# Row sums of squares by ScalarE's accumulating square on token-major loads, in a one-core decoder block

## The chip, the cores and the metric

The kernel runs on one core of a Trainium2 chip. The metric is the device time of one execution in microseconds (us). A core has five engines with queues of their own: PE (TensorE, matrix products), DVE (VectorE, elementwise), ACT (ScalarE, activations), POOL (GpSimd) and SP (which here only issues transfers). Transfers (DMA) are issued from SP, ACT or POOL and all run on the same 16 DMA engines. Each engine runs its instructions strictly in the order in which they stand in its queue.

## What is computed

One layer of a hybrid decoder block on 2048 tokens of 1024 channels: an RMS norm, one projection to 3080 columns, a pooling branch and a gated DeltaNet branch, an output projection with the residual, and a last RMS norm. The part that the change touches is the first norm:

```python
def rms_norm(x, w):
    xf = x.astype(jnp.float32)
    y = xf * lax.rsqrt(jnp.mean(xf * xf, axis=-1, keepdims=True) + NORM_EPS)
    return (y * w.astype(jnp.float32)).astype(x.dtype)

def reference(x, norm_w, w_in, ...):
    n = rms_norm(h, norm_w[layer])
    proj = jnp.einsum('bsd,de->bse', n, w_in[layer])
```

The scale of a token, one over the root of its mean square, is a factor of every projected column. So the kernel projects the unscaled x (times the norm's weight) and multiplies the scale into the results.

## The kernel before

**Tiling.** The tokens go in two blocks of 1024 (`b` = 0, 1), each in two halves of 512 (`hf` = 0, 1). x is loaded channel-major (`xT`: 128 channels on the partitions, 512 tokens along the row), as eight slices of a half in four transfers of 512 KB (`load_x`). Each slice, times the norm's weight, is split into a high part `nh` (rounded to the fast matmul type, on ACT) and a remainder `nl` (on DVE) by `split_x`. A projection (`project`) is eight steps `k`, each a triple of 512-column matmuls: `nh` and `nl` with the weight's high part `wh`, and `nh` with its low part `wl`. A projection of one weight tile over one half is 24 matmuls, a unit.

**Weights.** The first two weight tiles come with the first loads and are split on the engines. For each later tile POOL issues a transfer into `wh`, ACT makes a negated rounded copy in `wl` (L716), and POOL issues a second transfer that adds the weight to it (L717).

**The row scale.** `square_x` squares each slice on ACT; the squares are summed over the eight slices into `sacc`, the odd ones by DVE, the even ones by POOL (L533). `row_scale` then sums over the partitions: for each 128 tokens a matmul with one column of ones (`pss`, L538) puts the sum for each token on a partition. DVE adds the epsilon (`ms`, L542), POOL takes the power of -1/2 (`rstd`, L500), and DVE multiplies the 128x128 identity, which is loaded in `cst`, with each of the four scales (L549). `broadcast` multiplies these four diagonals by a matrix of ones (`psr`, L553): the scale of every token now stands on every partition, and ACT copies it to `rb` (L555). Every result of a projection is multiplied by `rb` when it leaves PSUM. A result that has no `rb` yet keeps its PSUM bank: three banks of pool `pp` and two of `pc` take the first five units.

**Gates.** Two more columns groups of the projection (`gate_rows`, `psba`) are scaled by `rb` on DVE (`ba`, L566) and transposed by PE (`tp`, L573), once for each half.

**What sets the order.** The program is traced in the order of slots that are written by hand (`at(slot, fn)`); the constants `L_...` are the offsets. A planner then lists all instructions again for each engine, with costs of its own for each operation and transfer (`costs`), and binds each engine to that order. Loads that are traced before `load_constants` are the opening: the planner sends them first, and reckons their landings one behind the other. SP keeps at most eight transfers under way: an issue waits until the eighth before it has landed.

The opening's loads on SP are the first half's `xT`, the weights, the second half's `xT`, and then the constants: `cst`, `wba` (the gate weights, from which `whl` is made), `pw`, and others.

Of the kernel before, what the change touches and what calls it, by code (L numbers as in the profile page):

```python
# [7 lines left out]
F32 = mybir.dt.float32  # L8
# [3 lines left out]
ALU = mybir.AluOpType  # L12
# [23 lines left out]
L_SPREAD, L_KK0 = 1.0, 4.5  # L36
L_CONV, L_SCAT, L_GAT, L_INV, L_FIN, L_POOL, L_GATE = 9, 8.4, 8.4, 28, 15.0, 12, 15
L_RB = (5.5, 4.25, 5.25, 4.25)
L_MIX, WARM = 90, 11
L_ROW, L_GROW, L_SUMS, L_DEC = 3.0, 2.5, 2, 4.0  # L40
L_KK, L_Q, L_QK, L_SPLIT, L_W = 1.5, 6.5, 1.5, 20, 30
L_ROW0, L_SQ1, L_SQB, L_X, L_GR0, L_GR, L_GCOL = (16.0, 18.0), 13.5, -40, 44, 21.5, 5.5, 2.75
# [44 lines left out]
class Planner:  # L87
# [34 lines left out]
    def costs(self, i, outs, ins):  # L122

        op, eng = i.opcode, i.engine.name
        n = 1
        for _, c in outs[0].bass_ap.ap[1:]:
            n *= c
        psum = any(a.bass_ap.tensor.name in self.psum for a in (*outs, *ins))
        if op == "DMACopy":
            kb = n * outs[0].bass_ap.ap[0][1] / 256  # L130
            if eng == "Pool":
                return 600, (2900 + 5.3 * kb if self.adds(i) else 2300 + 3.1 * kb)
            if type(outs[0].bass_ap.tensor).__name__ != "Tile" or outs[0].bass_ap.tensor.name.startswith(DRAM_TILES):
# [12 lines left out]
        if eng == "Activation":
            scaled = len(outs) > 1 or len(ins) > 1
            t = 170 + 0.6 * n if psum else 93 + 0.85 * n + 95 * scaled
            return t, t + 108
        if eng == "Pool":  # L150
            t = 600 if op == "TensorTensor" and n <= NC else {"TensorScalarAffineSelect": 620}.get(op, 0.95 * n if op == "Memset" else 2.5 * n + 20)
            return t, t + 30
        if op == "StreamTranspose":
            return 464, 450
        if op in ("TensorTensor", "TensorCopy"):
            t = 70 + 1.04 * n
        else:
            t = 125 + 1.05 * n if n >= P else 78 + n
        return t, t + 98
# [237 lines left out]
def hymba_kernel(  # L397
# [31 lines left out]
    def st(shape, dt, tag, bufs=1):  # L429
        return plan.tile(sp, shape, dt, tag, tag, bufs)  # L430
# [89 lines left out]
            out=nl[:, k], in0=xk, scalar=nw[:, k : k + 1], in1=nh[:, k], op0=ALU.mult, op1=ALU.subtract  # L520
        )

    def square_x(k, env):
        xk = env["x"][k // 2][:, k % 2]
        if k == 0:
            env["ss"] = ss = st([P, HALF], F32, "sacc", 2)
            nc.scalar.activation(ss, xk, AF.Square)
        else:
            ss = env["ss"]
            sq = st([P, HALF], F32, "acc", 3)  # L530
            nc.scalar.activation(sq, xk, AF.Square)
            eng = nc.vector if k % 2 else nc.gpsimd
            eng.tensor_tensor(out=ss, in0=ss, in1=sq, op=ALU.add)  # L533

    def row_scale(env):
        ps = plan.tile(pd, [P, HALF], F32, "pd", "pss", 2, True)
        for j in range(NCH):
            nc.tensor.matmul(  # L538
                ps[:, j : j + 1], env["ss"][:, j * P : (j + 1) * P], ones[:, 0:1], start=True, stop=True
            )  # L540
        v = st([P, NCH], F32, "ms", 2)
        nc.vector.tensor_scalar(  # L542
            out=v, in0=ps[:, 0:NCH], scalar1=1.0 / D, scalar2=EPS, op0=ALU.mult, op1=ALU.add
        )
        r = st([P, NCH], F32, "rstd", 2)
        rsqrt(r, v)
        env["dg"] = dg = st([P, NCH, P], F32, "sacc", 2)
        for j in range(NCH):
            nc.vector.tensor_scalar(out=dg[:, j], in0=ident, scalar1=r[:, j : j + 1], scalar2=None, op0=ALU.mult)  # L549
# [550 lines left out]
    for b in range(NB):  # L1100
# [21 lines left out]
        for hf in range(NHALF):  # L1122
            n[hf] = env = {}
            base = slot - (1 - hf) * 8 * PAIRED + 0.5
            for i in range(KT // 2):
                at(base - L_X if b else -79 + 8 * hf + i, load_x, b, hf, i, env)
            for k in range(KT):
                at(base + 0.1 + k * (8 * PAIRED - 2) / KT, split_x, k, env)
                at(base + (L_SQB if b else 4 + L_SQ1 * hf) + k * (8 * PAIRED - 2) / KT, square_x, k, env)
            base += 8 * PAIRED - 2  # L1130
            base += L_ROW if b else L_ROW0[hf]
            at(base, row_scale, env)
            at(base + L_RB[b * NHALF + hf], broadcast, env)
            env["slot"] = base + L_RB[b * NHALF + hf] + 0.1
        for hf in range(NHALF):
# [401 lines left out]
```

## Time and profile before

| | us |
|---|---|
| three timed runs | 944.51, 944.46, 942.41 (median 944.46) |
| the profiled execution | 943.07 |
| its span, first to last instruction | 941.4 |
| mean granted clock of PE | 0.996 |

Some of the costliest groups of instructions (line, engine, operation, out<-in, shapes, count, then busy us and mean ns):

```profile
L725 PE MATMUL ps<-nh,wh 128*128 128x512 f32 x768 | 325.8, 424 | 2.0 <-DVE sz L750 1.5
L716 ACT ACTIVATE wl<-wh 128x1024 fp32r<-128x1024 f32 x40 | 42.4, 1060 | 43.7 <-DMA wh<-in_w_in_dram 34.0
```

A group's last part is the idle time of the engine just before its instructions and what ended it. A wait's row names the instruction that waited, the one it waited for, and the microseconds in total, the number of times and the longest.

### The profile page before, as it was taken

The numbers are of one execution on the slowest core, as the hardware profiler recorded it, in microseconds if no ns is written. First come the engines' busy times: TensorE is split into PE (matmuls) and PEld (weight loads), VectorE is DVE, ScalarE is ACT, GpSimd is POOL, SyncE is SP. The second block draws the span as 40 slices with busy tenths as digits, with TensorE's granted clock in tenths as the row PEclk, the third lists the DMA queues.
The fourth block names the chain that finished last, engine by engine and source line by source line (L and its number), as shares of the span: only waits on it lengthen the run. The fifth ranks groups of instructions, "written<-read, shape, count | busy, mean of one in ns | idle before, by whom it ended". The sixth has DMA issues, their size and how long they took to land.

```text
span 941.4 us, 14710 instructions
## 1 busy us (share of the span) xinstructions
PE 916.7 (97%) x5226; PEld 739.4 (79%) x5226; DVE 618.2 (66%) x1637; ACT 467.0 (50%) x1209; POOL 187.5 (20%) x224
## 2 busy tenths in 40 slices
PE   8999999999999999999999999999999999999995
PEld 6678888878888877768877787888887788788884
DVE  7476867667758445855775775865844487976553
ACT  8348654464454245624944545545523435444442
POOL 3417210110111113312710121021011101012221
PEclk9999999999999999999999999999999999999998
DMA  8425574343433455434445344343248487376544
GB/s 291 103 60 108 135 170 109 63 99 87 96 100 75 134 168 151 95 74 90 95 96 123 63 91 95 73 101 98 63 110 255 127 229 227 127 187 163 152 111 123
DMA packets 82265, 115.81 MB, mean 123 GB/s; under 512 B 31888, under 2 KB 49552, under 8 KB 82192
## 3 DMA queue, kind: packets, MB, share of 16 engines
q0 software_dynamic: 17280, 56.89, 28.3%
q1 hardware_dynamic: 64480, 57.46, 19.9%
q8 instruction: 41, 0.67, 0.3%
q10 hardware_dynamic: 432, 0.53, 0.2%
q14 instruction: 32, 0.26, 0.1%
HBM read 92.83 MB, written 22.02 MB: 122 GB/s over the span
## 4 chain that ended last, share of the span: by engine, by line
PE 73%; issue 8%; DMA 6%; DVE 6%; POOL 2%; ACT 2%; SPq 1%; DVEq 0%; POOLq 0%; ACTq 0%
PE ps L725 14%; PE ps L727 14%; PE ps L726 14%; DMA wh<-in_w_in_dram 2%; PE psA L1391 2%; PE psA L1392 2%; PE psA L1390 2%; PE tp L817 2%; PE ch L1003 2%; PE ch L981 1%; PE ch L997 1%; PE ob L991 1%; PE ob L1007 1%; DMA dec<-in_xT_dram 1%; PE psC L1392 1%
## 5 line engine op out<-in xcount | busy, mean ns | idle before, releaser
L725 PE MATMUL ps<-nh,wh 128*128 128x512 f32 x768 | 325.8, 424 | 2.0 <-DVE sz L750 1.5
L726 PE MATMUL ps<-nl,wh 128*128 128x512 f32 x768 | 300.9, 392 | 2.2 <-DVE nl L519 2.2
L727 PE MATMUL ps<-nh,wl 128*128 128x512 f32 x768 | 301.5, 393 | 1.5 <-DMA wl<-in_w_in_dram 1.5
L727 PEld LDWEIGHTS ps<-nh,wl 128*128 128x128 f32 x768 | 144.2, 188 | 34.8 <-DMA wl<-in_w_in_dram 3.0
L725 PEld LDWEIGHTS ps<-nh,wh 128*128 128x128 f32 x768 | 145.0, 189 | 27.6 <-DVE sz L750 1.9
L726 PEld LDWEIGHTS ps<-nl,wh 128*128 128x128 f32 x768 | 145.2, 189 | 27.2 <-DVE nl L519 5.0
L739 DVE SCALAR_TENSOR_TENSOR acc<-u,cw,acc 128x512 f32<-128x512 f32 x144 | 109.7, 762 | 20.4 <-ACT acc L737 18.4
L708 POOL DMA_DIRECT2D wh<-in_w_in_dram x40 | 23.1, 578 | 295.2 <-PE ps L727 283.0
L734 DVE TENSOR_TENSOR u<-ps,rb 128x512 f32<-128x512 f32 x48 | 33.1, 689 | 56.5 <-PE ps L727 56.4
L717 POOL DMA_DIRECT2D wl<-in_w_in_dram x40 | 35.2, 880 | 163.8 <-ACT wl L716 116.6
L716 ACT ACTIVATE wl<-wh 128x1024 fp32r<-128x1024 f32 x40 | 42.4, 1060 | 43.7 <-DMA wh<-in_w_in_dram 34.0
L896 DVE TENSOR_TENSOR tmp<-Ai,X 128x60 f32<-128x60 f32 (+24 forms) x248 | 53.5, 216 | 9.4 <-DMA Ai<-blocks 3.1
L902 DVE TENSOR_TENSOR X<-X,tmp 128x60 f32<-128x60 f32 (+24 forms) x248 | 53.7, 216 | 6.6
L737 ACT ACTIVATE acc<-u,cw 128x512 f32<-128x512 f32 x48 | 34.9, 727 | 44.9 <-DVE u L734 43.9
L1010 ACT ACTIVATE sqj<-v 128x128 f32<-128x128 f32 x64 | 19.7, 308 | 62.2 <-DVE v L1008 61.0
L999 ACT ACTIVATE nv<-ch,sm 128x128 f32<-128x128 f32 x64 | 23.5, 368 | 33.9 <-PE ch L997 33.8
L1398 POOL DMA_DIRECT2D dec<-in_x_dram x23 | 20.2, 880 | 100.6 <-ACT dec L1397 58.9
L1004 DVE SCALAR_TENSOR_TENSOR state<-state,ex,ch 128x128 f32<-128x128 f32 x64 | 22.0, 344 | 22.1 <-PE ch L1003 21.2
L824 ACT ACTIVATE sqj<-tp 128x128 f32<-128x128 f32 x128 | 33.6, 278 | 4.4 <-PE tp L817 4.2
L993 ACT ACTIVATE o<-ob,ex 128x128 f32<-128x128 f32 x64 | 23.6, 369 | 20.4 <-PE ob L991 19.6
L1003 PEld LDWEIGHTS ch<-nv,kdec 128*128 128x128 f32 x128 | 19.6, 188 | 13.2 <-ACT nv L999 12.6
L750 DVE TENSOR_TENSOR szp<-ps,rb 128x512 f32<-128x512 f32 x16 | 11.0, 689 | 27.8 <-PE ps L727 27.8
(286 smaller groups left out, 1761.7 us busy)
## 6 DMA issues: line engine op xcount, KB each, us to landing
wh<-in_w_in_dram POOLq DMA_DIRECT2D x40, 512.0 KB, 4.0
wl<-in_w_in_dram POOLq DMA_DIRECT2D x40, 512.0 KB, 5.5
y_dram<-yt SPq DMA_DIRECT2D x32, 256.0 KB, 2.9
out_dram<-dec SPq DMA_DIRECT2D x14, 512.0 KB, 4.5
dec<-in_x_dram POOLq DMA_DIRECT2D x23, 256.0 KB, 4.1
Ai<-blocks SPq DMA_DIRECT2D x32, 128.0 KB, 2.7
yr<-y_dram SPq DMA_DIRECT2D x8, 512.0 KB, 4.4
dec<-in_xT_dram SPq DMA_DIRECT2D x7, 512.0 KB, 6.6
```

The source lines that it names most:

```text
L716: nc.scalar.activation(w["lo"], w["hi"].bitcast(F32), AF.Copy, scale=-1.0)
L717: nc.gpsimd.dma_start(w["lo"], w_in[et], accum_op=ALU.add)
L725: nc.tensor.matmul(ps, w["hi"][:, k], nh[:, k], start=(k == 0), stop=False)
L726: nc.tensor.matmul(ps, w["hi"][:, k], nl[:, k], start=False, stop=False)
L727: nc.tensor.matmul(ps, w["lo"][:, k], nh[:, k], start=False, stop=(k == KT - 1))
L734: nc.vector.tensor_tensor(out=ub[:, HALO:], in0=ps, in1=rb, op=ALU.mult)
L737: nc.scalar.activation(acc, ub[:, HALO:], AF.Copy, scale=cw[:, ci, CONV - 1 : CONV])
L739: nc.vector.scalar_tensor_tensor(out=acc, in0=ub[:, h0 + j : h0 + j + HALF], scalar=cw[:, ci, j : j + 1], in1=acc, op0=ALU.mult, op1=ALU.add,)
L824: nc.scalar.activation(junk, tp[:, j], AF.Square, accum_out=dst[:, c : c + 1])
L896: nc.vector.tensor_tensor(out=tmp[:, 0:n, 0:w], in0=Ai[:, j, j + 1 : BS].unsqueeze(1).to_broadcast([P, n, w]), in1=X[:, 0:n, j : j + 1].to ...
L902: nc.vector.tensor_tensor(out=X[:, 0:n, j + 1 : BS], in0=X[:, 0:n, j + 1 : BS], in1=tmp[:, 0:n, 0:w], op=ALU.subtract)
L1003: nc.tensor.matmul(ch[:, 2], e["kdec"][:, c], nv, start=True, stop=True)
```

## The change

The sums of squares are no longer made from the channel-major slices. x is loaded a second time, token-major: 128 tokens on the partitions and their 1024 channels along the row, 512 KB each (`load_rows`), four such loads for a half. ACT squares each in place and sums along the row in the same instruction (`square_rows`, `accum_out`), which leaves a token's sum on its partition, where the one-column matmul had put it. `square_x`, its additions and the matmuls `pss` are gone. `row_scale` keeps the epsilon and the power; the diagonals are a step of their own (`row_diagonal`).

In block 0 the row loads belong to the opening and use buffers that are free then (`ROW_TAGS`); one of them, `Ai`, is used by the first load of the first half and by the last of the second. In block 1 all eight go through one buffer (`yr1`), so each waits for the square of the one before. The slots are new too, and the planner's cost of a small power on POOL.

```diff
+ROW_TAGS = (
+    (("Ai",), ("At",), ("v0",), ("vT",)),
+    (("Tt", 2), ("Tt", 2), ("yr1",), ("Ai",)),
+)
...
-            t = 600 if op == "TensorTensor" and n <= NC else ...
+            t = 430 + 160 * n if op == "TensorTensor" and n <= NC else ...
...
-    def square_x(k, env):
-        xk = env["x"][k // 2][:, k % 2]
-        if k == 0:
-            env["ss"] = ss = st([P, HALF], F32, "sacc", 2)
-            nc.scalar.activation(ss, xk, AF.Square)
-        else:
-            ss = env["ss"]
-            sq = st([P, HALF], F32, "acc", 3)
-            nc.scalar.activation(sq, xk, AF.Square)
-            eng = nc.vector if k % 2 else nc.gpsimd
-            eng.tensor_tensor(out=ss, in0=ss, in1=sq, op=ALU.add)
+    def load_rows(b, hf, j, env):
+        env["xt", j] = xt = st([P, D], F32, *(ROW_TAGS[hf][j] if b == 0 else ("yr1",)))
+        t0 = b * TB + hf * HALF + j * P
+        nc.sync.dma_start(xt, x[t0 : t0 + P, :])
+
+    def square_rows(j, env):
+        if j == 0:
+            env["ms"] = st([P, NCH], F32, "ms", 2)
+        xt = env["xt", j]
+        nc.scalar.activation(xt, xt, AF.Square, accum_out=env["ms"][:, j : j + 1])
 
     def row_scale(env):
-        ps = plan.tile(pd, [P, HALF], F32, "pd", "pss", 2, True)
-        for j in range(NCH):
-            nc.tensor.matmul(
-                ps[:, j : j + 1], env["ss"][:, j * P : (j + 1) * P], ones[:, 0:1], start=True, stop=True
-            )
-        v = st([P, NCH], F32, "ms", 2)
...
+        v = env["ms"]
+        nc.vector.tensor_scalar(out=v, in0=v, scalar1=1.0 / D, scalar2=EPS, op0=ALU.mult, op1=ALU.add)
+        env["r"] = r = st([P, NCH], F32, "rstd", 2)
         rsqrt(r, v)
+
+    def row_diagonal(env):
         env["dg"] = dg = st([P, NCH, P], F32, "sacc", 2)
...
-                at(base + (L_SQB if b else 4 + L_SQ1 * hf) + k * (8 * PAIRED - 2) / KT, square_x, k, env)
...
-            at(base, row_scale, env)
+            for j in range(NCH):
+                at(base - L_XT + 4 * j if b else -70.5 + 8 * hf + 0.1 * j, load_rows, b, hf, j, env)
+                at(base - L_XT + 8 + 4 * j if b else 4 + 8 * hf + j, square_rows, j, env)
+            at(base - L_XT + 24 if b else base, row_scale, env)
+            at(base, row_diagonal, env)
             at(base + L_RB[b * NHALF + hf], broadcast, env)
```

What the planner makes of it shows in three places. First SP at the start of the program. Before (the names are those of the sections above; `dec`, `kdec`, `kT` are buffers that hold `xT` here, `qT` a weight):

```order
L703 DMA qT<-in_w_in_dram 128x512 x2
L513 DMA dec<-in_xT_dram 128x2x512
L513 DMA kdec<-in_xT_dram 128x2x512
L513 DMA kT<-in_xT_dram 128x2x512 x2
L481 DMA cst<-in_consts_dram 128x192
L481 DMA wba<-in_w_ba_dram 128x64
L481 DMA pw<-in_pool_w_dram 128x512
```

And with the change (its line numbers are those of the changed file; `in_x_dram` is x token-major):

```order
L703 DMA qT<-in_w_in_dram 128x512 x2
L517 DMA dec<-in_xT_dram 128x2x512
L530 DMA Ai<-in_x_dram 128x1024
L530 DMA At<-in_x_dram 128x1024
L530 DMA v_139<-in_x_dram 128x1024
L530 DMA vT<-in_x_dram 128x1024
L517 DMA kdec<-in_xT_dram 128x2x512
L517 DMA kT<-in_xT_dram 128x2x512 x2
L530 DMA Tt<-in_x_dram 128x1024 x2
L530 DMA yr_153<-in_x_dram 128x1024
L530 DMA Ai<-in_x_dram 128x1024
L485 DMA cst<-in_consts_dram 128x192
```

Four row loads stand between the first and the second load of the second half's `xT`, and four more between the last of these and `cst`.

Second, DVE in the opening. Before, from the first split of the second half on:

```order
L519 SCALAR_TENSOR_TENSOR nl<-dec,nw,nh 128x512 x2
L533 TENSOR_TENSOR sacc<-sacc,acc 128x512
L519 SCALAR_TENSOR_TENSOR nl<-kdec,nw,nh 128x512 x2
L519 SCALAR_TENSOR_TENSOR nl<-kT,nw,nh 128x512 x2
L542 TENSOR_SCALAR ms<-pss 128x4
L489 TENSOR_TENSOR whl<-wba,whl 128x8x8
L519 SCALAR_TENSOR_TENSOR nl<-kT,nw,nh 128x512 x2
L549 TENSOR_SCALAR sacc<-cst,rstd 128x128 x4
```

With the change:

```order
L523 SCALAR_TENSOR_TENSOR nl<-dec,nw,nh 128x512 x2
L540 TENSOR_SCALAR ms<-ms 128x4
L523 SCALAR_TENSOR_TENSOR nl<-kdec,nw,nh 128x512 x2
L523 SCALAR_TENSOR_TENSOR nl<-kT,nw,nh 128x512
L547 TENSOR_SCALAR sacc<-cst,rstd 128x128 x4
L523 SCALAR_TENSOR_TENSOR nl<-kT,nw,nh 128x512
L493 TENSOR_TENSOR whl<-wba,whl 128x8x8
L523 SCALAR_TENSOR_TENSOR nl<-kT,nw,nh 128x512
L763 TENSOR_TENSOR u<-ps,rb 128x512
```

The scale and the diagonals (`sacc<-cst,rstd`) have moved ahead of the last three splits. PE has 22 triples ahead of the first `psr` now, and had 21 and one group of `pss`. On POOL the first `wh` and `wl` transfers follow the first memsets now; before, an addition stood ahead of `wh`, and `wl` came behind three additions and the first power.

Third, DVE in block 1, up to the first `ba`. Before:

```order
L542 TENSOR_SCALAR ms<-pss 128x4
L770 TENSOR_TENSOR ps_s<-ps_s 128x513
L782 SCALAR_TENSOR_TENSOR acc<-ps_s,u 128x512
L549 TENSOR_SCALAR sacc<-cst,rstd 128x128 x4
L750 TENSOR_TENSOR szp<-ps,rb 128x512
L519 SCALAR_TENSOR_TENSOR nl<-dec,nw,nh 128x512 x2
L519 SCALAR_TENSOR_TENSOR nl<-kdec,nw,nh 128x512 x2
L519 SCALAR_TENSOR_TENSOR nl<-kT,nw,nh 128x512
L792 SCALAR_TENSOR_TENSOR yt<-acc,psc,szp 128x512
L519 SCALAR_TENSOR_TENSOR nl<-kT,nw,nh 128x512 x3
L566 TENSOR_TENSOR ba<-psba,rb 16x512
```

With the change:

```order
L770 TENSOR_TENSOR ps_s<-ps_s 128x513
L782 SCALAR_TENSOR_TENSOR acc<-ps_s,u 128x512
L750 TENSOR_TENSOR szp<-ps,rb 128x512
L523 SCALAR_TENSOR_TENSOR nl<-dec,nw,nh 128x512 x2
L523 SCALAR_TENSOR_TENSOR nl<-kdec,nw,nh 128x512 x2
L523 SCALAR_TENSOR_TENSOR nl<-kT,nw,nh 128x512
L792 SCALAR_TENSOR_TENSOR yt<-acc,psc,szp 128x512
L523 SCALAR_TENSOR_TENSOR nl<-kT,nw,nh 128x512 x3
L566 TENSOR_TENSOR ba<-psba,rb 16x512
```

The scale and the diagonals of this half are gone from this place; they stand some 60 rows earlier.

More of the change, by code (lines that the diff above doesn't have):

```diff
@@ L38 @@
 L_RB = (5.5, 4.25, 5.25, 4.25)
-L_MIX, WARM = 90, 11
+L_MIX, L_XT, WARM = 90, 60, 11
 L_ROW, L_GROW, L_SUMS, L_DEC = 3.0, 2.5, 2, 4.0
@@ L150, in costs @@
         if eng == "Pool":
-            t = 600 if op == "TensorTensor" and n <= NC else {"TensorScalarAffineSelect": 620}.get(op, 0.95 * n if op == "Memset" else 2.5 * n + 20)
+            t = 430 + 160 * n if op == "TensorTensor" and n <= NC else {"TensorScalarAffineSelect": 620}.get(op, 0.95 * n if op == "Memset" else 2.5 * n + 20)
             return t, t + 30
@@ L521, in split_x @@
         )
-    def square_x(k, env):
-        xk = env["x"][k // 2][:, k % 2]
-        if k == 0:
-            env["ss"] = ss = st([P, HALF], F32, "sacc", 2)
-            nc.scalar.activation(ss, xk, AF.Square)
-        else:
-            ss = env["ss"]
-            sq = st([P, HALF], F32, "acc", 3)
-            nc.scalar.activation(sq, xk, AF.Square)
-            eng = nc.vector if k % 2 else nc.gpsimd
-            eng.tensor_tensor(out=ss, in0=ss, in1=sq, op=ALU.add)
-    def row_scale(env):
-        ps = plan.tile(pd, [P, HALF], F32, "pd", "pss", 2, True)
-        for j in range(NCH):
-            nc.tensor.matmul(
-                ps[:, j : j + 1], env["ss"][:, j * P : (j + 1) * P], ones[:, 0:1], start=True, stop=True
-            )
-        v = st([P, NCH], F32, "ms", 2)
[L542 to L545, printed above, removed]
+    def load_rows(b, hf, j, env):
[7 more added lines that the diff above has]
+        nc.scalar.activation(xt, xt, AF.Square, accum_out=env["ms"][:, j : j + 1])
+    def row_scale(env):
+        v = env["ms"]
+        nc.vector.tensor_scalar(out=v, in0=v, scalar1=1.0 / D, scalar2=EPS, op0=ALU.mult, op1=ALU.add)
+        env["r"] = r = st([P, NCH], F32, "rstd", 2)
         rsqrt(r, v)
+    def row_diagonal(env):
         env["dg"] = dg = st([P, NCH, P], F32, "sacc", 2)
         for j in range(NCH):
-            nc.vector.tensor_scalar(out=dg[:, j], in0=ident, scalar1=r[:, j : j + 1], scalar2=None, op0=ALU.mult)
+            nc.vector.tensor_scalar(
+                out=dg[:, j], in0=ident, scalar1=env["r"][:, j : j + 1], scalar2=None, op0=ALU.mult
+            )
     def broadcast(env):
```

## The prediction

> **What bounds the kernel now.** The page comes first: busy times, then the chain that ended last.
>
> ```profile
> span 941.4 us, 14710 instructions
> PE 916.7 (97%) x5226; PEld 739.4 (79%) x5226; DVE 618.2 (66%) x1637; ACT 467.0 (50%) x1209; POOL 187.5 (20%) x224
> ...
> PE 73%; issue 8%; DMA 6%; DVE 6%; POOL 2%; ACT 2%; SPq 1%; DVEq 0%; POOLq 0%; ACTq 0%
> ```
>
> TensorE is busy for 97% of the span. Its instruction order is fixed, so work taken from it shortens the kernel, and work taken from the others does so only where TensorE waits. The list of TensorE's waits over the whole run says where:
>
> ```profile
> PE ps L726 <- DVE nl L519: 2.2, 5, 0.7
> PE tp L573 <- DVE ba L566: 1.9, 1, 1.9
> ```
>
> The first is the opening, where data arrives just in time. The second is the start of block 1. The change touches both places. So I read two stretches closely: 0 to 55 us and 389 to 410 us.
>
> **What leaves TensorE.** The one-column matmuls stand in the timeline as four groups. Two of them, one in each block, with the instruction that follows (start, duration):
>
> ```profile
> 22.16 0.94 PE L538 MATMUL pss<-ones,sacc 128*128 128x1 f32 x8
> 22.97 0.49 PE L725 MATMUL ps<-nh,wh 128*128 128x512 f32 x1
> ...
> 408.87 1.05 PE L538 MATMUL pss<-ones,sacc 128*128 128x1 f32 x8
> 409.78 0.48 PE L725 MATMUL ps<-nh,wh 128*128 128x512 f32 x1
> ```
>
> A group holds TensorE for 0.81 us (22.97 less 22.16) to 0.91 us; I take 0.81 for three and 0.91 for the last. All four would be 3.3 us if nothing else moved.
>
> **What the added loads do in the opening.** The queue of SP is the place to look. Windows of 4 to 16 us (columns: length, busy of PE, PEld, DVE, ACT, POOL, clock, DMA share, GB/s), and the issue and time to landing of the constants `cst`:
>
> ```profile
> 4.00:16.00 12.00, 9.92 (x38) 6.43 (x37) 9.61 (x14) 10.36 (x18) 2.30 (x2) 1.00 1.05 389
> ...
> 8.79 0.34 SPq L481 DMA_DIRECT2D cst<-in_consts_dram  x1
> cst<-in_consts_dram SPq DMA_DIRECT2D x1, 96.0 KB, 8.4
> ```
>
> The DMA engines are full (share 1.05) at 389 GB/s. The 96 KB of `cst` take 8.4 us because they land behind everything issued earlier: 8.79 + 8.4 = 17.2 us. In the changed order eight loads of 512 KB rows stand ahead of `cst`. They move 8 x 0.524 MB = 4.19 MB, and 4.19 / 0.389 = 10.8 us. Two transfers of POOL's queue also come before it now. Their rows:
>
> ```profile
> 14.20 0.75 POOL L708 DMA_DIRECT2D wh<-in_w_in_dram  x1
> ...
> 25.84 0.91 POOL L717 DMA_DIRECT2D wl<-in_w_in_dram  x1
> ...
> 27.00:32.00 5.00, 5.00 (x20) 2.81 (x21) 3.32 (x10) 3.90 (x7) 0.39 (x1) 1.00 0.75 133
> ```
>
> `wh` was issued at 14.20, behind an addition on POOL; with the additions gone it follows the memsets. Its 0.52 MB cost the others at most 0.52 / 0.389 = 1.3 us, and part of it overlapped `cst` already: +1.0. `wl` was issued at 25.84, after `cst`; it now follows ACT's first row square and so comes before it. At the full rate it costs 1.3 us. The window 27 to 32, which holds it and little else, shows 0.75 x 5 = 3.75 us of all engines for 0.67 MB, so up to 3.0 us for 0.52 MB. I take 1.9, nearer to the full-rate row because that one is from a full queue.
>
> `cst` lands at 17.2 + 10.8 + 1.0 + 1.9 = **30.9 us**, between 29.5 (both at 1.3 or less, rows a little faster) and 32.3 (1.3 and 3.0).
>
> The Trainium skill, "DMA: Bandwidth & Descriptors", section Specifications, gives about 358 GB/s as the limit of HBM for one core. At that figure the rows would take 11.7 us (an estimate from that page), 0.9 more. The 389 GB/s measured here is above it, so the measurement decides.
>
> **Who waits for `cst`.** The identity in `cst` is multiplied by the row scale into four diagonals, and these feed `psr`, the broadcast matmul:
>
> ```profile
> 25.90 0.89 DVE L549 TENSOR_SCALAR sacc<-cst,rstd 128x128 f32<-128x128 f32 x4 [0.27 <-POOL rstd L500]
> 26.94 1.10 PE L553 MATMUL psr<-sacc,ones 128*128 128x512 f32 x2 [0.26 <-DVE sacc L549]
> ...
> 53.31 0.39 PE L725 MATMUL ps<-nh,wh 128*128 128x512 f32 x1
> 53.54 0.39 PE L726 MATMUL ps<-nl,wh 128*128 128x512 f32 x1
> 53.76 0.39 PE L727 MATMUL ps<-nh,wl 128*128 128x512 f32 x1
> 54.08 0.42 PE L573 MATMUL tp<-cst,ba 16*128 16x16 f32 x4
> ```
>
> Before, the diagonals waited 0.27 us for `rstd` from POOL, with `cst` long there. Now the row scale is early and `cst` is late. `psr` follows the first diagonal by 26.94 - 25.90 = 1.04 us, so it starts at 30.9 + 1.04 = 31.9. Behind the diagonals on DVE stand three of the `nl` splits, `whl` and the first product with `rb`. On ACT, `whl<-wba` waits for the next constant, with a split, a square and the `rb` copy behind it. TensorE waits for all of these, but after `psr`, and they are 0.2 to 0.8 us each while `psr` and the three triples behind it run.
>
> TensorE has 22 triples (three matmuls of 512 columns) ahead of `psr` now, and had 21 and a `pss` group. Its matmuls start 0.23 us apart (53.31, 53.54, 53.76), so a triple takes 0.68 us. I compare at `tp`, the second transpose of gate rows, which has 43 triples ahead of it in both kernels. Before: 54.08 - 26.94 = 27.14 us from `psr` to it. Now one triple and one `pss` group fewer: 27.14 - 0.68 - 0.81 = 25.65, so 31.9 + 25.65 = 57.6. **Term 1: +3.5 us** (+2.1 to +4.9 by the bounds). The squares on ACT do not add to it: the four rows of the first half land ahead of the second half's `xT`.
>
> **The clock.** TensorE runs out of work at 21 to 26 us (22 triples from 6.06 on are 15 us, and its waits for `nl` add some), so it stands idle for 6 to 11 us. Rows of the end and of the start show what that does:
>
> ```profile
> 930.87 0.40 PE L1392 MATMUL psA<-Ai,wl 128*128 128x512 f32 x1
> 932.00:934.00 2.00, 0.00 (x0) 0.00 (x0) 0.90 (x3) 1.85 (x5) 0.00 (x0) 0.96 0.00 0
> 934.00:936.00 2.00, 0.00 (x0) 0.00 (x0) 1.61 (x4) 0.41 (x3) 1.60 (x2) 0.50 0.00 0
> ...
> 1.13 4.75 PE L465 MATMUL warm<-ones 128*128 128x128 f32 x22 [1.13 <-DVE mhalf L460]
> ...
> 6.39 0.40 PE L726 MATMUL ps<-nl,wh 128*128 128x512 f32 x1
> 6.79 0.50 PE L727 MATMUL ps<-nh,wl 128*128 128x512 f32 x1
> 7.21 0.50 PE L725 MATMUL ps<-nh,wh 128*128 128x512 f32 x1
> ...
> 10.25 0.39 PE L727 MATMUL ps<-nh,wl 128*128 128x512 f32 x1
> 10.48 0.40 PE L725 MATMUL ps<-nh,wh 128*128 128x512 f32 x1
> ```
>
> After the last matmul the granted clock falls to 0.50 within 3 us. At the start the matmuls follow each other in 0.40 and 0.42 us until 7.21, and in 0.23 by 10.48. The clock column reads 1.00 there all the same, so I go by the steps: TensorE was slow for 6.1 to 9.3 us from its first matmul at 1.13, and slow steps take twice the time: 3.0 to 4.6 us lost. After a gap in mid-run the price lies between 0 (the gate stays open) and 4.6; the nearest row says 3.0, the middle is 2.3. **Term 2: +2.7 us.**
>
> The Trainium skill, "TensorE: Matmul & The Clock Gate", Part 1, speaks against the change here: the clock halves after an idle window of about 3.4 us and opens after a busy one, windows that run freely. By that page the loss would be 1.7 to 3.4 us (an estimate), and the sum +2.6 to +4.3. The trace agrees with the fall; no run before shows a reopening in mid-run.
>
> **Block 1.** Two `pss` groups go: -(0.81 + 0.91) = **-1.7 us, term 3**. The wait of 1.9 us at `tp` follows DVE, which is full there:
>
> ```profile
> 388.03 0.69 DVE L533 TENSOR_TENSOR sacc<-sacc,acc 128x512 f32<-128x512 f32 x1
> 389.00:407.00 18.00, 17.62 (x78) 11.97 (x77) 17.72 (x32) 9.93 (x15) 4.38 (x5) 1.00 0.43 105
> ...
> 400.44 0.88 DVE L549 TENSOR_SCALAR sacc<-cst,rstd 128x128 f32<-128x128 f32 x4 [0.21 <-POOL rstd L500]
> ...
> 407.79 0.67 DVE L566 TENSOR_TENSOR ba<-psba,rb 16x512 f32<-16x512 f32 x1
> ```
>
> From 389 to 407 DVE is busy 17.72 of 18 us. Of that queue, the change takes the addition at 388.03 (0.6 net of overlap), the scale and diagonals around 400 with the wait of 0.21 (1.1), so `ba` comes 1.7 earlier. TensorE also arrives 0.81 earlier, without its `pss` group, so only 0.9 of the wait goes; the rest is late still, for the `nl` splits in the same queue. **Term 4: -0.9 us** (0 to -1.9). The eight row loads of this block are spread over the stretch before it, whose window reads:
>
> ```profile
> 330.00:385.00 55.00, 53.61 (x324) 42.19 (x323) 28.60 (x66) 27.95 (x72) 13.94 (x14) 1.00 0.57 157
> ```
>
> They need 10.8 us of DMA, and 0.43 x 55 = 24 us are free; their squares stand on an ACT that is busy for half (27.95 of 55). I cost them at nothing; without that cover each would cost its 1.35 us of DMA (rival 3). The additions taken from POOL and DVE elsewhere, and four more table loads on ACT, lie beside TensorE's work.
>
> **Sum.** 3.5 + 2.7 - 1.7 - 0.9 = +3.6 us. The profiled execution took 943.07 us (span 941.4 and 1.7 around it), so it becomes 946.7; I give 946.6. The median shown, 944.46, is 1.4 above that execution, so a comparison side by side should read the +3.6 (0.4%), and the absolute number may be 1 higher.
>
> **Rivals.**
> 1. *The clock does not fall, or the gap is short.* For it: DMA may run at 400 GB/s and the gate was seen to close only at the end. Against: a gap of 6 us is twice what the end needed. Then the sum is 3.5 - 2.6 = +0.9: 944.0.
> 2. *Not slower: the constants do not queue behind the rows.* Place: SP's queue between the rows and `cst`. Its price: if `cst` lands before about 23 us, `psr` starts when the 22 triples are through, about 24.5; then `tp` is at 24.5 + 25.65 = 50.2, -3.9, and with block 1 the sum is -6.5: 936.6. It decides from a landing before 27.3 us on with the clock loss, 30.0 without it: there the sum is zero. Against: 8.4 us for 96 KB shows the queue is served in order.
> 3. *The rows of block 1 collide.* Each row load puts 1.35 us (0.524 / 0.389) ahead of a weight or of a head's gather. If TensorE waits for two or three of these, +3 to +4 more: 950.
>
> **How the numbers follow.** Forecast 0.60, its own range 944 to 949; rival 1 0.17; rival 2 0.10; rival 3 0.13. About 0.3% (2.8 us) can be told from no change. The forecast's +3.6 is just above it, so 0.38 of its 0.60 counts as slower and 0.22 as the same; rival 3 adds 0.13 to slower; rival 1 adds 0.17 to the same. Slower 0.51, same 0.39, faster 0.10. The range leaves out rival 2 and the upper end of rival 3: 942.5 to 951.
>
> **What would show it.** In the profile after: `cst` landing at 29.5 to 32.3; TensorE's longest wait at `psr`, on the diagonals, of 5 us or more; steps of 0.4 us behind it and a clock under 1.00 in those windows; the second `tp` of gate rows at about 60; the wait at `tp` in block 1 under 1.2 us. The forecast is wrong if `cst` lands before 25, or if TensorE waits in block 1 for row squares or weights.

## The result, and the profile after

The median of ten runs went from 944.49 to 948.14 us: 1.0040 times the time before, with a 95% interval of 1.0026 to 1.0054. That is +3.65 us; the sum of the prediction was +3.6, its time 946.6. The total came out as forecast, but, as the runs below show, not by the terms of the forecast alone.

The page of the changed kernel, busy times and the chain that ended last:

```profile
span 946.3 us, 14618 instructions
PE 913.7 (97%) x5194; PEld 738.7 (78%) x5194; DVE 603.8 (64%) x1621; ACT 472.2 (50%) x1213; POOL 170.1 (18%) x212
...
PE 72%; issue 10%; DMA 8%; ACT 4%; DVE 3%; POOL 1%; SPq 1%; DVEq 0%; POOLq 0%; ACTq 0%
```

TensorE has 3.0 us less to do (913.7 for 916.7) and the span is 4.9 us longer, so about 8 us more of waiting. (The 4.9 is more than the 3.65 of the medians, because the profiled execution of the kernel before was 1.4 us under its median.) The list of TensorE's waits over the whole run has four new heads:

```profile
PE psr L553 <- DVE sacc L547: 6.8, 1, 6.8
PE ch L1003 <- ACT nv L999: 3.0, 2, 2.3
PE ps L727 <- DMA wl<-in_w_in_dram: 2.8, 4, 1.3
PE ps L725 <- ACT nh L522: 1.9, 1, 1.9
```

The first and the last are the opening; the second and most of the third lie between 345 and 400 us, ahead of block 1. The wait of 1.9 us at `tp` on `ba` is gone.

**The opening.** The list of transfers gives the time of `cst` from issue to landing, the timeline the rest (start, duration, and in brackets the idle time ahead and what ended it):

```profile
cst<-in_consts_dram SPq DMA_DIRECT2D x1, 96.0 KB, 11.9
```

```profile
20.26 0.33 SPq L485 DMA_DIRECT2D cst<-in_consts_dram  x1
...
21.91 1.04 POOL L504 TENSOR_TENSOR rstd<-ms,mhalf 128x4 f32<-128x4 f32 x1 [2.21 <-DVE ms L540]
...
26.01 0.39 PE L727 MATMUL ps<-nh,wl 128*128 128x512 f32 x1
32.29 0.88 DVE L547 TENSOR_SCALAR sacc<-cst,rstd 128x128 f32<-128x128 f32 x4 [7.79 <-DMA cst<-in_consts_dram]
33.22 2.08 PE L553 MATMUL psr<-sacc,ones 128*128 128x512 f32 x2 [6.83 <-DVE sacc L547]
...
59.75 0.42 PE L573 MATMUL tp<-cst,ba 16*128 16x16 f32 x4
```

The row scale was ready at 23.0; the diagonals waited for the identity until 32.2 (20.26 + 11.9); TensorE stood from 26.4 to 33.2. The second `tp` of gate rows is 5.7 us later than before (59.75 for 54.08). The windows (clock, DMA share and GB/s at the end of each row) show the queue and the clock:

```profile
16.00:20.00 4.00, 4.00 (x19) 3.30 (x18) 1.29 (x2) 4.00 (x7) 0.88 (x1) 1.00 1.03 399
20.00:24.00 4.00, 4.00 (x20) 3.30 (x19) 1.78 (x4) 3.97 (x8) 1.04 (x1) 1.00 1.06 367
24.00:28.00 4.00, 2.40 (x11) 1.66 (x9) 0.50 (x1) 1.05 (x2) 0.00 (x0) 1.00 1.05 315
28.00:30.00 2.00, 0.00 (x0) 0.00 (x0) 0.00 (x0) 0.00 (x0) 0.00 (x0) 0.87 1.00 396
30.00:32.00 2.00, 0.00 (x0) 0.00 (x0) 0.00 (x0) 0.00 (x0) 0.00 (x0) 0.50 0.85 266
...
34.00:36.00 2.00, 2.00 (x5) 1.05 (x4) 0.67 (x2) 1.00 (x4) 0.95 (x1) 0.50 0.00 0
36.00:38.00 2.00, 2.00 (x10) 1.43 (x9) 2.00 (x4) 2.00 (x5) 0.95 (x1) 0.93 0.00 0
```

The DMA engines are full until 30 us; from 20 to 28, with the accumulating `wl` transfer in flight (18.8 to 27.4 us), they move 367 and then 315 GB/s at the same share at which they moved 399 before. The clock falls to 0.50 at 29.5 and is back at 36.3, 3.1 us after TensorE resumed.

**Block 1.** The timeline of ACT, SP and TensorE ahead of block 1, and the row of the same load in the chain of waits:

```profile
344.67 1.04 ACT L536 ACTIVATE yr<-yr 128x1024 f32<-128x1024 f32 x1
...
346.04 2.25 SPq L530 DMA_DIRECT2D yr<-in_x_dram  x1
...
356.15 1.06 ACT L536 ACTIVATE yr<-yr 128x1024 f32<-128x1024 f32 x1 [2.01 <-DMA yr<-in_x_dram]
357.11 0.19 ACT L536 ACTIVATION_READ_ACCUMULATOR yr<-yr 128x1 f32 x1
357.20 0.35 ACT L999 ACTIVATE nv<-ch,sm 128x128 f32<-128x128 f32 x1
357.61 0.49 PE L1003 MATMUL ch<-nv,kdec 128*128 128x128 f32 x2 [2.26 <-ACT nv L999]
```

```profile
346.04 10.03 DMA yr<-in_x_dram
```

The row load issued at 346.04 took 10.0 us to land. Its square stood at the head of ACT's queue meanwhile; `nv`, which TensorE needed, stood behind it. The DMA engines there, after and before:

```profile
337.00:352.00 15.00, 12.59 (x110) 9.25 (x109) 4.93 (x13) 6.98 (x17) 3.00 (x4) 1.00 1.04 314
```

```profile
330.00:345.00 15.00, 13.91 (x120) 10.59 (x119) 5.12 (x11) 7.00 (x18) 1.99 (x3) 1.00 0.86 239
345.00:360.00 15.00, 15.00 (x87) 12.16 (x86) 10.14 (x26) 8.33 (x25) 2.57 (x2) 1.00 0.12 40
```

Before, a stretch with share 0.86 was followed by one with 0.12. The planner's row loads fell into the first.

**Where the time goes.** The 2304 projection matmuls (rows `ps` of the timeline) come in both kernels in nearly the same order. Taking the start of the n-th one in this kernel less that in the kernel before gives a running lateness. Here it is for the changed kernel and all experiments, at the times that the kernel before shows (us):

| | 54 | 161 | 333 | 379 | 439 | 630 | 773 | median, ratio to before [95%] |
|---|---|---|---|---|---|---|---|---|
| changed | +5.7 | +7.1 | +7.2 | +11.8 | +8.3 | +5.8 | +5.1 | 948.14, 1.0040 [1.0026, 1.0054] |
| e1 | -2.8 | -2.0 | -2.1 | +2.1 | -0.6 | -3.1 | -3.8 | 943.27, 0.9983 [0.9967, 0.9999] |
| e11 (as e1) | -3.1 | -3.5 | -3.4 | +1.7 | -1.2 | -2.7 | -3.4 | 939.99, 0.9952 [0.9931, 0.9974] |
| e2 | +5.9 | +5.4 | +5.5 | +5.6 | +4.3 | +1.1 | +0.5 | 945.48, 1.0013 [0.9999, 1.0026] |
| e3 | +0.2 | +0.5 | +0.3 | +4.9 | +0.8 | -2.6 | -2.8 | 938.94, 0.9935 [0.9919, 0.9951] |
| e4 | +7.1 | +8.3 | +8.5 | +11.3 | +8.8 | +5.5 | +4.9 | 946.69, 1.0020 [1.0007, 1.0032] |
| e5 | -0.5 | -0.5 | -0.4 | 0.0 | +0.1 | -0.4 | -0.9 | 942.57, 0.9981 [0.9971, 0.9991] |
| e6 | +4.6 | +3.9 | +4.1 | +10.5 | +8.1 | +4.7 | +4.3 | 946.76, 1.0023 [1.0009, 1.0037] |
| e7 | -2.6 | -1.8 | -1.4 | -0.7 | -2.2 | -5.3 | -5.9 | 937.22, 0.9926 [0.9908, 0.9944] |
| e8 | +6.9 | +6.2 | +6.1 | +12.5 | +9.6 | +6.6 | +5.9 | 951.20, 1.0066 [1.0050, 1.0083] |
| e9 | -2.0 | -1.6 | -2.2 | +4.1 | -0.1 | -3.4 | -4.1 | 937.81, 0.9925 [0.9904, 0.9946] |
| e10 | -2.9 | -2.2 | -2.3 | -1.6 | -0.3 | -3.6 | -4.3 | 937.63, 0.9924 [0.9897, 0.9950] |
| e12 | +6.3 | +7.2 | +7.6 | +12.1 | +9.2 | +6.8 | +6.3 | 949.07, 1.0059 [1.0042, 1.0076] |

The lateness is of one profiled execution; the medians are of 5 to 12 runs of each kernel, whose times spread over 3 to 7.5 us. Each ratio is to runs of the kernel before that were made beside it, with medians of 944.0 to 945.2. e1 and e11 are the same kernel, and their ratios differ by 0.3%; so a smaller difference between two rows of the last column says little. One run of e4 took 1509.65 us at a granted clock of 0.555; it is left out of the ratio. The changed kernel loses 7.1 us in the first 161 us, 4.6 from 333 to 379, gets 3.5 back by 439 and 3.2 behind it.

### The profile page after: what moved, and what is told of

Same layout as the page of the kernel before. It is cut to its first block, busy times and chain, and to the rows that moved or that the text cites. A ratio compares the mean times of both kernels' runs of the same rounds, so it can differ in the third digit from the quotient of the medians.

```text
span 946.3 us, 14618 instructions
## 1 busy us (share of the span) xinstructions
PE 913.7 (97%) x5194; PEld 738.7 (78%) x5194; DVE 603.8 (64%) x1621; ACT 472.2 (50%) x1213; POOL 170.1 (18%) x212
## 4 chain that ended last, share of the span: by engine, by line
PE 72%; issue 10%; DMA 8%; ACT 4%; DVE 3%; POOL 1%; SPq 1%; DVEq 0%; POOLq 0%; ACTq 0%
PE ps L725 14%; PE ps L727 13%; PE ps L726 13%; PE ch L1003 2%; PE psA L1394 2%; DMA yr<-in_x_dram 2%; PE psA L1395 2%; PE psA L1393 2%; PE tp L817 2%; PE ch L981 2%; PE ob L991 1%; PE ob L1007 1%; PE ch L997 1%; DMA cst<-in_consts_dram 1%; PE psC L1395 1%
## 5 line engine op out<-in xcount | busy, mean ns | idle before, releaser
L993 ACT ACTIVATE o<-ob,ex 128x128 f32<-128x128 f32 x64 | 23.6, 369 | 19.9 <-PE ob L991 18.8
L1003 PE MATMUL ch<-nv,kdec 128*128 128x128 f32 x128 | 27.8, 299 | 3.1 <-ACT nv L999 3.0
```

The lines of the kernel that those rows point to most:

```text
L1003: nc.tensor.matmul(ch[:, 2], e["kdec"][:, c], nv, start=True, stop=True)
```

## The experiments

**e1: the constants ahead of the rows.**

```diff
+    def load_identity():
+        nc.sync.dma_start(cst, consts[:, 0:C_TMP])
+        nc.sync.dma_start(wba, w_ba)
...
+    at(-70.6, load_identity)
```

> The changed kernel with cst and wba issued ahead of the eight row loads; the order of TensorE, DVE and POOL is otherwise kept. Theory (the opening is lost because the identity stands behind 4.2 MB of rows in SP's queue): the rows' 22 triples end at about 26.4, psr starts there instead of 33.2, the clock stays at full speed behind it, the second tp of gate rows starts at 52 to 53 instead of 59.75; total 7 to 8 us under the changed kernel's 948.1, 939.5 to 942. Rival (the rows' volume itself is what is paid, through the second half's xT and the weights): TensorE waits as long for something else, the second tp stays past 57, total 945 or more.

Measured: `cst` was issued at 5.69 and landed 9.3 us later, at 15.0, and the wait at `psr` vanished:

```profile
25.21 1.02 PE L555 MATMUL psr<-sacc,ones 128*128 128x512 f32 x2
...
51.31 0.42 PE L575 MATMUL tp<-cst,ba 16*128 16x16 f32 x4
```

The second `tp` is 8.4 us earlier than in the changed kernel, and it and `psr` come about 1 us sooner than expected. (Against the kernel before, `tp` is 2.8 us sooner; rival 2 of the prediction, which is this case, put 3.9.) The eight rows move as many bytes as they did; only the identity's place in SP's queue is other. The rival falls: the opening's loss is the queue. The time was 943.3 where at most 942 was expected; the twelve runs lay in two groups, 937.7 to 939.6 and 943.2 to 945.1.

**e2: rows in block 0 alone**, the sums of block 1 by `square_x` and `pss` as before.

```diff
+                if b == 1:
+                    at(base + (L_SQB if b else ...) + ..., square_x, k, env)
...
-            for j in range(NCH):
+            for j in range(NCH if b != 1 else 0):
```

> The changed kernel with the sums of block 1 made as before (slices, additions, one-column matmuls), rows in block 0 alone. Theory (row loads of block 1 cost 4 to 5 us between 330 and 400 us, and the rest of block 1 gives 3.4 back at 400 to 430): TensorE is 7 us later than before at 200 us and still 7 to 8 later at 400 and at 430, without the extra 4 us between 330 and 400; total 948 to 951. Rival (my prediction: block 1's row loads are free): the same lateness at 200 us, and at 430 it is 2.6 us later than the changed kernel is there (8.3 + 2.6 = 10.9), because the pss groups and the wait on ba come back and nothing else goes.

Measured: lateness 5.5 at 333 us, 5.6 at 379, 4.3 at 439. The 4.6 us of the changed kernel between 333 and 379 are not there. By the medians, block 1's rows cost the changed kernel 2.7 us (948.14 less 945.48; by the ratios 0.27%, close to what two rows of the table can differ by without a cause), and by the lateness 4.0 at 439; the prediction had them as a gain of 2.6. The time was below the range expected, since here too 3.8 us are won behind 439.

**e3: rows in block 1 alone**, the same edit for block 0.

> The changed kernel with the sums of block 0 made as before, rows in block 1 alone. Theory: no loss in the opening (second tp at 54 to 55), 4 to 5 us lost between 330 and 400, 3.4 won back by 430; total 942 to 946, no more than 2 us from the kernel before. Rival (prediction: block 1 gains 2.6): 941.9 and no loss between 330 and 400.

Measured: no loss in the opening, 4.6 between 333 and 379, 4.1 won back by 439, 3.6 behind it. The median of 938.94 is below the range: the block-1 part by itself makes the kernel 0.65% faster, and on top of the rows of block 0 (the changed kernel against e2) it makes it slower. The stretch from 333 to 379 loses as much in both. More than half of the difference lies behind 439: there 3.8 us are won with rows in block 0 alone (e2), 3.6 with rows in block 1 alone, and 3.2 with both, so once and not twice. The row loads do not fall at the same place either: the last one is issued at 357.1 here and at 370.9 in the changed kernel, which at that point is 7 us late, so some 7 us sooner relative to the work.

**e4: short row loads in block 1.**

```diff
-        nc.sync.dma_start(xt, x[t0 : t0 + P, :])
+        w = 8 if b else D
+        nc.sync.dma_start(xt[:, 0:w], x[t0 : t0 + P, 0:w])
...
+            eight = xt[:, 0:8].unsqueeze(1).to_broadcast([P, 127, 8])
+            nc.scalar.activation(xt[:, 8:]..., eight, AF.Square, accum_out=acc)
```

> The changed kernel with each row load of block 1 cut to 8 columns, which the square then reads 127 times, so that its ACT time and the order on every engine stay the same; the scale of block 1 is left wrong by this. Theory (late landing of the loads and their bandwidth cost TensorE the 4 to 5 us between 330 and 400): the waits at ch on nv (3.0) and at ps on wl (2.1 + 1.2) fall under 1.5 together, total 943 to 945. Rival (the squares' own ACT time, 8 x 1.04 us in front of nv): the waits stay, total 947 or more.

Measured, TensorE's waits from 330 to 390 us:

```profile
PE ps L735 <- DMA wl<-in_w_in_dram: 2.5, 2, 1.8
PE xx L956 <- issue: 0.4, 1, 0.4
PE ch L1011 <- ACT nv L1007: 0.3, 1, 0.3
```

The wait on `nv` went from 3.0 to 0.3 with the squares' ACT time kept, so the late landing made it, and not the square alone. The load of 4 KB that stands where the changed kernel's took 10.0 us still took 7.7:

```profile
yr<-in_x_dram SPq DMA_DIRECT2D x1, 4.0 KB, 7.7
```

Most of that landing time is therefore what lies ahead of the load, and not its own bytes. The waits on `wl` did not go, and the total improved by 1.5 us of the 3 to 5 expected. TensorE, no longer held at 355, came to the weight at 380 sooner and waited there. Half of the theory holds (the landing), half does not (that the loads' bandwidth makes the waits on `wl`).

**e5: the planner's cost line alone, on the kernel before.**

```diff
-            t = 600 if op == "TensorTensor" and n <= NC else ...
+            t = 430 + 160 * n if op == "TensorTensor" and n <= NC else ...
```

> The kernel before with one line of the change alone: the planner's cost of a small power on POOL (430 + 160 n ns instead of 600). No row loads. Theory: this line makes the 3 us that the changed kernel and every variant run so far win between 440 and 760 us (after: late by 8.3 at 439 and by 5.1 at the last projection matmul), so TensorE is level with the kernel before up to 400 us and 3 to 3.6 ahead of it at the end; total 940.5 to 941.5. Rival (that gain comes from the sums that are made otherwise): 943.5 to 944.5, no gain behind 440.

Measured: 0.19% faster (1.8 us), of which the lateness shows 0.5 in the opening and 1.0 behind 439. So the line is worth something, but a third of the 3.2 us that it was to explain behind 439.

**e6: TensorE kept busy in the gap.**

```diff
+        if not hot:
+            hot.append(plan.tile(pd, [P, HALF], F32, "pd", "hot", 2, True))
+            for i in range(28):
+                nc.tensor.matmul(hot[0][:, 0:P], ones, ones, start=True, stop=True)
         ps = plan.tile(pd, [P, HALF], F32, "pd", "psr", 2, True)
```

> The changed kernel with 28 matmuls of ones on TensorE ahead of the first psr, in the gap in which it waits for the identity; their result is used by nothing and every other order is kept. Theory (the clock's fall in that gap costs 1.5 us behind it): no slow window at 30 to 36, steps of 0.23 behind psr, the second tp at 58 to 58.5 instead of 59.75, total 946 to 947. Rival (the steps behind psr are slow for want of splits from DVE): tp stays at 59.75, total 948.

Measured, in the timeline and in the window of 34 to 36 us:

```profile
27.46 6.41 PE L559 MATMUL hot<-ones 128*128 128x128 f32 x56
33.70 1.02 PE L561 MATMUL psr<-sacc,ones 128*128 128x512 f32 x2
...
58.71 0.42 PE L581 MATMUL tp<-cst,ba 16*128 16x16 f32 x4
```

```profile
34.00:36.00 2.00, 2.00 (x9) 1.36 (x8) 1.47 (x5) 1.78 (x4) 0.96 (x1) 1.00 0.01 0
```

With work in the gap the clock reads 1.00 at 34 to 36 us, and from `psr` to the second `tp` it is 25.0 us (58.71 - 33.70) for 26.5 (59.75 - 33.22) in the changed kernel. The clock's fall costs 1.5 us. The rival falls. (`tp` itself, at 58.71, is 0.2 us above the range expected: the added matmuls end at 33.87 and hold `psr` back by 0.5.)

**e7: e1 and e2 together** (rows in block 0 alone, constants first).

> Rows in block 0 alone (block 1 by slices, as in the kernel before) and the constants ahead of the rows. By the lateness of the two runs that did one of these each (2.2 ahead at 330 us, 1.2 won from 330 to 440, 3.8 behind it): span 934, total 935 to 938. Theory on the two groups of times of the first experiment (938 to 939.6 and 943.2 to 945): they come from the five idle stretches of 0.8 to 1.7 us of TensorE at 334 to 374, which close the clock in some executions; without rows in block 1 these are gone and the times form one group under 939. Rival: they come from the idle of 1.9 us at 8 us in the opening, which this kernel keeps: two groups again, 5 us apart.

Measured: 937.22, 0.74% faster than the kernel before, with a lateness near to what the two single edits promised (-1.4 at 333 us, -0.8 more by 439, -3.7 behind it). The six runs lie between 935.2 and 940.2, in one group, though one of them is above the 939 that was expected.

**e8: short squares in block 1.**

```diff
+        xt = xt[:, 0:8] if b else xt
-        nc.scalar.activation(xt, xt, AF.Square, accum_out=...)
+        nc.scalar.activation(xt, xt, AF.Square, scale=128**0.5 if b else 1.0, accum_out=...)
```

> The changed kernel with the squares of block 1 cut to the first 8 columns (times 128, so the scale of block 1 is an estimate from 8 channels), the row loads and every order kept: 8 x 0.9 us of ACT go. Theory (the late landing of a row holds ACT's queue): the wait of 2 us or more at ch on nv stays at 355, total 946 to 948. Rival (the squares' own time): nv's waits go below 0.5, total 943 to 945. The wl waits that stayed with short loads (3.9 us): below 1.5 if the squares' time in front of the negated copies makes them, else as before.

Measured: neither. `nv` waited 0.7 (2 or more, or under 0.5, were expected), the waits on `wl` rose to 6.0, and the kernel was slower than the changed one (951.2). The late row load is still there: issued at 345.39 us, it takes 9.2 us, and ACT waits 1.3 us for it, where it waited 2.0 in the changed kernel:

```profile
354.71 0.21 ACT L538 ACTIVATE yr<-yr 128x8 f32<-128x8 f32 x1 [1.28 <-DMA yr<-in_x_dram]
```

But the square behind it is 0.8 us shorter, and the landing takes 0.8 us less. So the 2.3 us at `nv` in the changed kernel are the landing and the square together, and both expectations have a part of it. Then TensorE waits for the `wl` at 380 instead, 3.6 us here, and the clock is at half speed from 383.6 to 387.0 behind that wait.

**e9: constants first, and block 1's rows 50 us earlier.**

```diff
+        for k in range(N):
+            if id(L[k]) in self.early:
+                late[k] -= 50000
```

> Constants ahead of the rows, rows in both blocks, and the planner told that block 1's row loads and squares are due 50 us sooner, so that they fall at 270 to 330 us, where the kernel without them (e7) moves little. Theory (a row load costs by where it lands, not by itself): no wait at ch on nv over 0.5 between 330 and 380, the stretch 330 to 440 gives back 2 us or more (e1: loses 1.5) and the total is 936 to 938 in one group, against 943 for e1. Rival (eight more loads and squares cost 4 to 5 us wherever they stand): the waits move to 270 to 330 and the total stays at 942 or more.

Measured: 937.81, in the range, with no wait on `nv` between 330 and 390. The rival's time of 942 or more does not come. By the medians the kernel is as fast as with the old sums in block 1 (e7), and 2 to 5 us faster than with the rows where the planner put them (e11, e1). But e11 and e1 are one kernel, the interval of e9 overlaps that of e11, and the profiled executions of the three lie within 0.8 us (938.75, 939.48, 939.02): that the quiet stretch makes it faster is not shown. The stretch from 333 to 439 was to give back 2 us or more; it loses 2.1, as e11 does (2.2): 6.3 are lost by 379, and 4.2 won back. Its waits:

```profile
PE ps L739 <- DMA wl<-in_w_in_dram: 6.5, 2, 4.5
```

The longer one is for the `wl` issued at 365.99 us, which lands 9.9 us later. In e7 it takes 6.8. SP's queue in e9 and POOL's in e7:

```profile
365.32 0.37 SPq L523 DMA_DIRECT2D kdec<-in_xT_dram  x1
365.78 0.42 SPq L523 DMA_DIRECT2D dec<-in_xT_dram  x1
```

```profile
365.92 0.88 POOL L744 DMA_DIRECT2D wl<-in_w_in_dram  x1 [4.52 <-ACT o L1020]
```

In e9 two slices of block 1's `xT` are issued just ahead of `wl`; in e7 these go out at 366.70 and 367.16, just behind it. That order is the difference I can see; it was not tried by itself. The other traces speak for it: in e3 the two loads stand 1.5 and 1.1 us ahead of the same transfer, which takes 8.7 us, and in the twelve profiles in which they follow it, it takes 6.2 to 7.8 in eleven and 8.5 in one (e8). It is the same weight for which e3, e4, e6 and e8 wait 3.0, 1.8, 2.4 and 3.6 us.

**e10: the first weight held back**, on e7.

```diff
+        nc.gpsimd.tensor_tensor(out=st([P, 4], F32, "e"), in0=xk, in1=mhalf[:, 0:4], op=ALU.add)
```

> e7 with one more instruction: a small addition on POOL that reads the last slice of the first half's xT and stands ahead of the first weight transfer in POOL's queue, so that this transfer is issued behind the landing of that slice (about 12 us) and no longer at 1.3 to 2.6 us. Every other order is kept. Theory (the early weight transfer, 0.52 MB, delays the first half's xT: TensorE's wait of 1.8 us at ps on nh at 8.5 us, which then closes the clock from 10 to 13.5): that wait falls under 0.6, no slow window before 20 us, total 1.5 to 3.5 under e7, 933.5 to 936. Rival (the weight is then late for the split and the fifth unit): a wait of 1 us or more on wl at 30 to 40 us and no gain.

Measured: the weight's transfer went from 1.42 to 10.93 us and the wait on `nh` at 8.5 disappeared, as expected, with no slow window before 20 us. A wait of the same size came in its place:

```profile
23.36 0.50 PE L764 MATMUL ps<-nh,wh 128*128 128x512 f32 x1 [1.79 <-ACT nh L533]
```

It comes from the weight that was held back, by way of ACT's queue:

```profile
18.52 1.06 ACT L755 ACTIVATE wl<-wh 128x1024 fp32r<-128x1024 f32 x1 [2.73 <-DMA wh<-in_w_in_dram]
...
22.60 1.32 ACT L533 ACTIVATE nh<-kdec,nw 128x512 fp32r<-128x512 f32 x2
```

`wh` lands at 18.5 us (8.7 in e7), ACT stands 2.7 us for it, and three row squares follow before the `nh` that TensorE needs, whose `xT` had landed at 21.1, 0.6 us sooner than in e7. So the wait moves and the time stays (937.63 for 937.22). The gain expected was wrong; the rival (the weight is late for the split) is nearer, though TensorE waits at 22 us and for `nh`, and not on `wl`.

**e11: e1 once more.**

> e1 once more, for a second profiled execution: its first one belonged to the faster group (938 to 939.6 of 12 times, the others at 943.2 to 945). Theory: an execution of the slower group has the same waits within 0.5 us, and two or three slow windows of the clock of 3.4 us or 6.8 us behind the idle stretches at 8 us or at 334 to 376 us. Rival: no slow window more, and a wait somewhere that is 4 us longer.

Measured: 939.99, five runs from 938.9 to 942.0, so the profiled one was not of the upper group of e1. Its waits are those of e1 within 1.2 us, and it has two slow windows of 3.4 us (10.6 to 14.0 and 334.8 to 338.3) where e1 had none before its end. That the clock's windows differ between executions of one kernel is shown; that they make e1's two groups is not.

**e12: the changed kernel with the old cost line.**

> The changed kernel with the planner's old cost of a small power on POOL (600 ns); TensorE, SP and POOL keep their order, ACT and DVE change places in some 15 rows. Theory (the line is worth about 1 us behind 440 us, as it was by itself): level with the changed kernel up to 440 us, about 1 us later at the last projection matmul (6 behind the kernel before instead of 5.1), total 948.5 to 950. Rival (the line brings all the 3.4 us that the changed kernel wins back behind 440): 8.5 behind, 951 to 952.

Measured: 949.07, 0.9 us over the changed kernel, and 6.3 behind at the end: the size expected. But 0.65 of it is in the opening (at 54 us), and it wins 2.9 us behind 439, nearly as much as the changed kernel. From 333 to 379 it loses 4.5 us, though its wait on `nv` there is 0.6 and not 3.0. So the gain behind 439 is not the cost line's.

## Why the prediction came out as it did

**Term 1, the late identity: right in cause, 0.7 too small.** `cst` landed at 32.2, at the upper end of 29.5 to 32.3. The row loads ran at 395 to 399 GB/s until 20 us, near the 389 reckoned. The accumulating `wl` was mis-sized: 1.9 us was taken. From 20 to 28 us the rows of 367 and 315 GB/s fall 0.46 MB short of 399, which is 1.2 us beside the 1.3 of its own bytes: 2.5, an estimate from these windows. The other 0.7 of the 1.3 us by which `cst` was later than 30.9 was not traced. `psr` started at 33.2 for 31.9, and from there to `tp` it took 25.0 (e6) for 25.65. With the clock taken off (e6), the second `tp` is 4.2 us late (5.7 - 1.5) for the +3.5 of the sum. e1 shows that the cause is the queue.

**Term 2, the clock: right in kind, 1.2 too large.** +2.7 was put, +1.5 measured by e6. The loss was taken from the start of the kernel, where TensorE works from the first microsecond of the slow stretch; here over half of the slow stretch (29.5 to 36.3) lies in the gap itself and costs nothing. The estimate from the Trainium skill, "TensorE: Matmul & The Clock Gate", Part 1, was 1.7 to 3.4; what e6 measured is just below it.

**Terms 3 and 4, block 1: right in size, but not all there was.** The `pss` groups are gone, and so is the whole wait on `ba` (1.9 where 0.9 was put). Together that is 3.6, near the 3.5 us won between 379 and 439. The agreement is rough: two waits on `wl` of 1.2 us in all are new in the same stretch, and e2 and e7, which keep the `pss` groups, win 1.3 and 1.5 there.

**"I cost them at nothing": the step that failed.** The row loads and squares of block 1 were set against mean shares: 24 us of free DMA in 55, an ACT busy for half. Both means hide where the loads fall. Eight loads on one buffer are a chain, the planner put one into a stretch that was full already, its landing took 10.0 us where the planner's `costs` reckon 5.9, and ACT stood still with `nv` in its queue. Rival 3, which had 0.13 and +3 to +4, named the collision and the weights that come late by it, but not the way through ACT's queue; the stretch lost 4.6. That the rows are the cause is shown by e2 and e7, which have none in block 1 and lose 0.1 and 0.7 there. By e2 the block-1 part as a whole costs the changed kernel 2.7 us instead of gaining 2.6. What in them is costly is not settled. The wait on `nv` is nearly gone in e4, e8, e9 and e12, and the stretch still loses 2.8 to 6.4 us. TensorE's waits on `wl` from 325 to 439 us sum to 2.5 to 6.5 us in the nine profiles with rows in block 1, whether the loads are short (e4), the squares are short (e8) or both come 50 us sooner (e9), and to 0.9 to 1.9 in the five without; what makes those weights late was not separated.

**What made up for it.** Some 3 us (2.2 to 4.1) are won behind 439 us by the changed kernel and by every variant with rows, and the prediction had nothing there. TensorE's waits from 439 us to the last projection matmul sum to 4.4 us before and to 1.7 in the changed kernel. The two largest, before:

```profile
PE ps L725 <- DVE sz L750: 1.5, 1, 1.5
PE ch L997 <- DVE rho L983: 1.4, 2, 1.2
```

At 534 us `rho` stood in DVE's queue behind a sum that waited 1.5 us for a gather (`Ai<-blocks`); in the changed kernel that gather is there in time, and the wait is gone. At 491, `sz` stood in DVE's queue behind a long row of small operations; that wait is 1.0 in the changed kernel and 0.3 to 0.5 in e1, e2, e6 and e7. Why DVE is sooner there was not traced. The cost line gives about 1 by itself (e5), but the gain is there without it too (e12), and in kernels that are late (e2) as in kernels that are early (e7). What brings the gain stays open. In the other direction, 1.4 us that the changed kernel loses from 54 to 161 us were not predicted either; e6, which differs from it only in the gap, does not lose them.

So the opening was right for its reasons (+6.2 forecast, 5.7 at 54 us), and the sum was right by luck: in block 1 a gain of 2.6 was forecast and 1.1 lost (333 to 439 us), a missing cost of 3.7, and the missing gain behind it was 3.2. Of the signs named ahead, the landing, the wait at `psr`, the slow steps, the second `tp` (59.75) and the wait on `ba` came as said; the one that was to show the forecast wrong, TensorE waiting ahead of block 1 for squares and weights, came too.

## What to carry over

An added load is priced at the place in the queue where it is issued, by what stands behind it: 96 KB of constants behind 4.2 MB of rows cost more here than everything that the change saved, and with them ahead the change is 0.2 to 0.5% faster than the kernel before (e1, e11), with rows in block 0 alone 0.7% (e7). A mean share of free time says nothing about a chain of transfers on one buffer; look at the windows of 5 to 15 us in which each of them would land, and at what its consumer's queue holds behind it. When a wait is taken away, look for the next late thing on the same stretch: the `wl` at 380 us took back most of what e4, e8 and e9 had won.

## What the runs showed of the hardware

The clock's slow stretches ahead of the end were 3.41, 6.83 or 10.24 us long in all twelve profiles that had one, and idle stretches of TensorE well below 3.4 us were followed by one in some executions and not in others (start and length of the idle stretch, and the slow window behind it, us):

```
changed   8.45  1.88   12.40 to 15.81
e7        8.46  1.75   10.04 to 13.45
e6        8.12  2.47   10.02 to 16.85
e1        8.19  1.91   none
e2        8.40  1.72   none
before  406.66  1.86   none
e5      406.29  0.76  409.75 to 413.16
e11     332.90  0.97  334.83 to 338.25
e10     405.38  1.24  408.43 to 411.84
e12     350.28  1.34  351.79 to 355.20
e3      373.80  3.03  375.82 to 382.65
e9      371.46  4.51  376.81 to 380.22
e8       26.69  6.59   28.64 to 38.88
```

The Trainium skill, "TensorE: Matmul & The Clock Gate", Part 1, has the clock set by an activity window of about 3.4 us that runs freely; the lengths agree. It speaks of idle gaps of more than about 3.4 us; here stretches of 0.76 to 1.34 us in mid-run were followed by a slow window, and one of 1.86 was not. (The rows at 8 us are less clean: the steps of the first matmuls are slow until about 10 us in the kernel before, with the clock column at 1.00.)

The accumulating weight transfer of 512 KB lands 5.6 us after its issue in the median of the changed kernel's 40. One and the same of them took 9.9 us with two 512 KB loads issued within 0.7 us ahead of it (e9), 8.7 with these 1.5 and 1.1 us ahead (e3), and 6.2 to 8.5 in the twelve profiles in which they follow.

In a stretch in which the DMA engines are full, a load of 4 KB took 7.7 us to land (e4) where one of 512 KB took 10.0 (changed); in quieter stretches they took 1.6 and 3.5.
